# A hybrid decoder step: four buffers for raw weight blocks instead of three, and 64 tile slots instead of 66

## The chip, the cores and the metric

The kernel runs on one core of a Trainium2 chip. The metric is device time in microseconds of one execution; three executions of the kernel before took 2662.25, 2661.33 and 2662.22 us, so the median is 2662.22. The core has five engines with a queue each: TensorE (PE, with its weight loads shown as PEld), VectorE (DVE), ScalarE (ACT), GpSimd (POOL) and SyncE (SP). SP does nothing here but issue transfers; POOL issues a second stream of them.

## The reference

One layer of a decoder trunk in float32. The 512 tokens of a prompt and 8 tokens of a decode batch go through it together (520 columns in the kernel); d_model is 2048.

```python
def block(x, rg_h, rg_conv, C, n, m, ml_conv, mk, mv, w):
    y, new = mixer(rmsnorm(x, w['g_mix']), rg_h, rg_conv, C, n, m, ml_conv, w)
    x = x + y.astype(x.dtype)
    x = x + cross_attn(rmsnorm(x, w['g_xattn']), mk, mv, w).astype(x.dtype)
    hf = rmsnorm(x, w['g_ffn'])
    x = x + (jnp.square(jax.nn.relu(hf @ w['w_up'])) @ w['w_down']).astype(x.dtype)
    return x, new
```

The mixer multiplies by w_in (2048 x 5128) and feeds eight heads of a gated linear recurrence (RNN) and four heads of an mLSTM with a matrix state C (256 x 256 for each head; decode has a state of its own for each of 8 sequences), then multiplies by w_out. Cross-attention has four heads over 256 memory tokens: the prompt's keys and values are the memory times w_mk and w_mv, those of decode come from a cache (K, V). The feed-forward part has 8192 hidden columns: w_up, squared ReLU, w_down. Outputs are the two y and all the new states.

## The kernel before, in words

**Blocks and jobs.** All weights are cut into blocks of 128 partitions x 8 x 128 float32, 512 KB each. A list `jobs` has an entry for each product with a block. A float32 block is used as two halves: `whi`, cast to the type fp32r by ScalarE (line 129, or 138 where the order is written by hand), and `wlo`, block minus `whi`, by VectorE (line 130 or 146). The matmuls of a job are made three times, whi by xh, whi by xl, wlo by xh. So each job of w_in has 48 matmuls of 260 columns (line 205), a job of w_mk 24 (line 1100), and one of w_mv 12 of 512 columns (line 1131).

**How a block arrives.** `w_raw` (line 106) takes a raw buffer from `wpool` (line 60, three buffers for each tag) and has SP load the block (line 108). `run_jobs` (line 164) goes through the jobs: at job i it asks for the raw blocks of later jobs (`w_load`), for the blocks of a group of products five jobs ahead (`w_fetch`, FETCH = 5), makes the two halves for job i+2, steps through the running tasks (pieces of vector work between the matmuls), and then issues the matmuls of job i. SP's queue is in order: a load for which no raw buffer is free makes everything behind it wait.

**Groups of seven products.** w_out, w_co, w_up and w_down are taken four blocks at a time (A11, A12, A21, A22) with seven products instead of eight, from sums of blocks (`form`, line 1303) and sums of activations; their jobs (`quad_jobs`, matmuls in line 1333) use `fetch0` and `fetch1` to load A11 and A12 by `w_raw` and A21 and A22 into another pool of five buffers (line 1291). There a raw buffer comes free when VectorE has formed the last sum that reads it or the low half of it.

**Slots.** Nearly all other tiles of the size of an activation (up to 524 float32 for each partition) share one pool of slots (`slots`, SLOTS buffers). Activations of the hidden layer are written to memory (`hc`, lines 1362 and 1363) and read back in w_down (`ha`, `hact_load`, line 1506) together with the residual X (line 1534).

**Order of work.** Three stretches are in the order in which the program is written (`manual_schedule`): the prologue with the first 10 jobs, the w_cq, w_mk and w_mv jobs with cross-attention and the first w_co jobs (about 745 to 1220 us), and the end. All others are put in order by the framework's scheduler, with a priority that `tc.high_priority(offset=AHEAD)` raises for loads and halves. The stages in time: w_in with RNN and mLSTM to about 590 us; w_out to 745; w_cq to 940; w_mk and w_mv with attention to about 1170; w_co to about 1350 (with a gap at 1207 to 1216, where it waits for the attention of decode); w_up to about 1990; w_down to about 2640; the final norm.

**Lines that the text names.** RNN gates: matmuls in line 730, sigmoid `g` in 731, its tanh and exp in 735 and 736. mLSTM of the prompt: 656 and 659 (numerator and denominator), 663 (state update), 667 (state C on VectorE), 673 (`rd`, absolute value of the denominator). mLSTM decode: `ct`, scaled on ScalarE in 574 and stored as output. Attention: 224 (three-pass products), 1182 (p), 1195 (transpose of p), 1087 (`mvl`, low half of values), 1137 (`mv` from PSUM), 1138 (its store), 987 (decode's cached V, loaded by POOL), 799 (`to`, from which w_co is multiplied).

Of the kernel before, what the change touches and what calls it, by code (L numbers as in the profile page):

```python
# [9 lines left out]
F32 = mybir.dt.float32  # L10
# [7 lines left out]
P = 128  # L18
# [6 lines left out]
EPS = 1e-6  # L25
FF = 8192
NMEM = 256
SLOTS = 66
SLOT = 524

C_MIX, C_X, C_FFN, C_FIN, C_MEM = 0, 16, 32, 48, 64
# [14 lines left out]
def tile_trunk(ctx: ExitStack, tc: tile.TileContext, a, o):  # L46
# [3 lines left out]
    const = ctx.enter_context(tc.tile_pool(name="const", bufs=1))  # L50
    slots = ctx.enter_context(tc.tile_pool(name="slots", bufs=SLOTS))
    wpool = ctx.enter_context(tc.tile_pool(name="wpool", bufs=3))
# [11 lines left out]
    def nm(s):  # L64
        uid[0] += 1
        return f"{s}_{uid[0]}"
# [37 lines left out]
    tasks = []  # L104

    def w_raw(src):
        raw = wpool.tile([P, 8, P], F32, tag="wraw", name=nm("wraw"))
        load(raw, src)
        return raw

    def w_load(i):
        if "fetch" in jobs[i] or "raw" in jobs[i] or "w" in jobs[i]:
            return
        jobs[i]["raw"] = w_raw(jobs[i]["src"])

    def w_fetch(i):
        if i < len(jobs) and "fetch" in jobs[i]:
            jobs[i]["fetch"]()
# [22 lines left out]
    def w_low(i):  # L141
        if "w" in jobs[i]:
            return
        raw, hi = jobs[i].pop("cast")
        lo = wpool.tile([P, 8, P], F32R, tag="wlo", name=nm("wlo"))
        V.tensor_tensor(out=lo, in0=raw, in1=hi.bitcast(F32), op=ALU.subtract)  # L146
        jobs[i]["w"] = hi, lo
# [5 lines left out]
    def step_tasks(cost=1.0):  # L153
        for t in list(tasks):
            t[2] += 1.0 if t[1] is None else t[1] * cost
            while t[2] > 0.999:
                t[2] -= 1.0
                try:
                    next(t[0])
                except StopIteration:  # L160
                    tasks.remove(t)
                    break

    def run_jobs(first, last, fixed=False, low_first=False):


        n = len(jobs)
        for i in range(first, last):
            with tc.high_priority(offset=AHEAD):
                for k in (i + 3, i + 4)[1 if i else 0:]:  # L170
                    if k < n:
                        w_load(k)
                w_fetch(i + FETCH)
                if i + 2 < n:
                    (w_cast if fixed else w_split)(i + 2)
            j = jobs[i]
            if "pre" in j:
                j["pre"]()
            if low_first:
                w_low(i + 2)  # L180
            step_tasks(j.get("cost", 1.0))
            if fixed and i + 2 < n:
                w_low(i + 2)
            j["mm"](*j.pop("w"))
            if "post" in j:
                with tc.high_priority(offset=EVAC):
                    j["post"]()
        while last == n and tasks:
            step_tasks()
# [1092 lines left out]
    def quad_jobs(srcs, acts, nacc, evac, order=None, early=False):  # L1282
# [11 lines left out]
        def fetch0():  # L1294
            q["A11"] = w_raw(srcs[0])
            q["A21"] = raw2("A21", srcs[2])

        def fetch1():
            q["A12"] = w_raw(srcs[1])
            q["A22"] = raw2("A22", srcs[3])  # L1300
# [349 lines left out]
    with tc.manual_schedule():  # L1650
        prologue()
        run_jobs(0, EARLY)
    run_jobs(EARLY, n_cq)
    with tc.manual_schedule():
        run_jobs(n_cq, n_early + 2, True)
        while tasks:
            step_tasks()
# [117 lines left out]
```

## Time and profile before

| | |
|---|---|
| median of three executions | 2662.22 us |
| the profiled execution | 2666.71 us |
| its span | 2664.9 us |
| mean granted TensorE clock | 0.995 |
| TensorE matmuls busy | 2625.3 us (99%) |
| VectorE busy | 2222.9 us (83%) |
| ScalarE busy | 1297.3 us (49%) |
| read from memory, written | 434.26 MB, 103.59 MB |

The profile is of one execution. Busy time counts an engine's instructions; "waits" are idle stretches of an engine, put down to what ended them; the chain is the work that ended last, followed back. Matmuls overlap one another, so a matmul's own duration (some 280 to 400 ns) is longer than the distance between two of them.

### The profile page before, as it was taken

The numbers are of one execution on the slowest core, as the hardware profiler recorded it, in microseconds if no ns is written. First come the engines' busy times: TensorE is split into PE (matmuls) and PEld (weight loads), VectorE is DVE, ScalarE is ACT, GpSimd is POOL, SyncE is SP. The second block draws the span as 40 slices with busy tenths as digits, with TensorE's granted clock in tenths as the row PEclk, the third lists the DMA queues.
The fourth block names the chain that finished last, engine by engine and source line by source line (L and its number), as shares of the span: only waits on it lengthen the run. The fifth ranks groups of instructions, "written<-read, shape, count | busy, mean of one in ns | idle before, by whom it ended". The sixth has DMA issues, their size and how long they took to land.

```text
span 2664.9 us, 52682 instructions
## 1 busy us (share of the span) xinstructions
PE 2625.3 (99%) x21250; PEld 2588.0 (97%) x21250; DVE 2222.9 (83%) x3733; ACT 1297.3 (49%) x1783; POOL 125.5 (5%) x216
## 2 busy tenths in 40 slices
PE   9999999999999999998999999999999999999997
PEld 9999999999999988988999999999999999999997
DVE  6787685897865567879999999999999988998898
ACT  5646455553453145545565555555553333333344
POOL 0010010000001212320000000000000000000001
PEclk9999999999999999999999999999999999999999
DMA  5354343566455778886686565565579666555642
GB/s 199 111 183 155 112 167 102 177 221 236 141 186 200 272 269 274 293 282 221 219 273 242 199 211 183 199 211 185 197 244 329 217 222 217 185 171 186 214 129 89
DMA packets 241926, 541.17 MB, mean 203 GB/s; under 512 B 25630, under 2 KB 97982, under 8 KB 241682
## 3 DMA queue, kind: packets, MB, share of 16 engines
q1 hardware_dynamic: 221202, 466.42, 51.6%
q0 software_dynamic: 20480, 71.38, 7.8%
q8 instruction: 167, 2.74, 0.4%
q14 instruction: 77, 0.63, 0.1%
HBM read 434.26 MB, written 103.59 MB: 202 GB/s over the span
## 4 chain that ended last, share of the span: by engine, by line
PE 89%; DVE 5%; DMA 3%; issue 2%; ACT 1%; POOL 0%; SPq 0%; POOLq 0%; ACTq 0%; DVEq 0%
PE mm L1333 53%; PE mm L205 22%; PE mm L1100 3%; PE aux L1333 2%; PE aux L224 2%; PE mm L1131 2%; PE mm L1376 2%; DVE wlo L130 1%; DMA wraw<-in_w_mv 1%; ACT whi L129 0%; PE aux L730 0%; DVE wlo L146 0%; DMA hc<-r 0%; PE aux L663 0%; PE aux L659 0%
## 5 line engine op out<-in xcount | busy, mean ns | idle before, releaser
L129 ACT CAST whi<-wraw 128x1024 fp32r<-128x1024 f32 x396 | 416.1, 1051 | 637.0 <-PE mm L1333 422.9
L1333 PE MATMUL mm<-ha,whi 128*128 128x260 f32 x3584 | 643.7, 283 | 2.2 <-DVE X L1514 1.2
L130 DVE TENSOR_TENSOR wlo<-wraw,whi 128x1024 fp32r<-128x1024 f32 x396 | 483.6, 1221 | 121.4 <-ACT whi L129 116.1
L1333 PEld LDWEIGHTS mm<-ha,whi 128*128 128x128 f32 x3584 | 551.2, 188 | 3.1 <-DVE X L1514 1.6
L1333 PE MATMUL mm<-ha,wlo 128*128 128x260 f32 x1792 | 505.1, 282 | 0.5 <-DVE wlo L130 0.5
L1333 PE MATMUL mm<-ta,whi 128*128 128x260 f32 x2320 | 419.3, 283 | 0.0
L1333 PEld LDWEIGHTS mm<-ta,whi 128*128 128x128 f32 x2320 | 355.6, 188 | 0.1
L1333 PEld LDWEIGHTS mm<-ha,wlo 128*128 128x128 f32 x1792 | 336.9, 188 | 1.0 <-DVE wlo L130 0.9
L1333 PE MATMUL mm<-ta,wlo 128*128 128x260 f32 x1160 | 326.4, 281 | 0.0
L1333 PE MATMUL mm<-fa,whi 128*128 128x260 f32 x1488 | 269.8, 283 | 0.0
L205 PE MATMUL mm<-xh,whi 128*128 128x260 f32 x1280 | 265.2, 288 | 0.0
L205 PE MATMUL mm<-xl,whi 128*128 128x260 f32 x1280 | 259.3, 284 | 0.0
L205 PE MATMUL mm<-xh,wlo 128*128 128x260 f32 x1280 | 258.3, 283 | 0.0
L129 ACT CAST whi<-A 128x1024 fp32r<-128x1024 f32 x140 | 146.9, 1050 | 195.3 <-PE mm L1333 123.3
L1333 PEld LDWEIGHTS mm<-fa,whi 128*128 128x128 f32 x1488 | 229.2, 189 | 0.0
L138 ACT CAST whi<-wraw 128x1024 fp32r<-128x1024 f32 x100 | 105.1, 1051 | 239.0 <-PE mm L205 79.4
L1333 PEld LDWEIGHTS mm<-ta,wlo 128*128 128x128 f32 x1160 | 218.5, 188 | 0.0
L1333 PE MATMUL mm<-fa,wlo 128*128 128x260 f32 x744 | 209.7, 282 | 0.0
L1514 DVE TENSOR_TENSOR X<-mm,X 128x260 f32<-128x260 f32 x448 | 171.0, 422 | 41.4 <-PE mm L1333 38.7
L205 PEld LDWEIGHTS mm<-xh,whi 128*128 128x128 f32 x1280 | 198.7, 189 | 1.4
L205 PEld LDWEIGHTS mm<-xh,wlo 128*128 128x128 f32 x1280 | 198.4, 189 | 0.2
L205 PEld LDWEIGHTS mm<-xl,whi 128*128 128x128 f32 x1280 | 198.0, 189 | 0.4
(435 smaller groups left out, 5217.2 us busy)
## 6 DMA issues: line engine op xcount, KB each, us to landing
ha<-hc SPq DMA_DIRECT2D x224, 260.0 KB
wraw<-in_w_in SPq DMA_DIRECT2D x80, 512.0 KB
wraw<-in_w_up SPq DMA_DIRECT2D x66, 512.0 KB
wraw<-in_w_down SPq DMA_DIRECT2D x64, 512.0 KB
A<-in_w_down SPq DMA_DIRECT2D x64, 512.0 KB
A<-in_w_up SPq DMA_DIRECT2D x62, 512.0 KB
hc<-hhi SPq DMA_DIRECT2D x32, 910.0 KB
hc<-r SPq DMA_DIRECT2D x32, 910.0 KB
```

What stands on the lines that cost most here:

```text
L129: S.copy(hi, raw)
L130: V.tensor_tensor(out=lo, in0=raw, in1=hi.bitcast(F32), op=ALU.subtract)
L138: S.copy(hi, raw)
L205: PE.matmul(ps[:, hf, 0:HT], w[:, j, :], x[:, HALF[hf]], start=(k == 0 and wi == 0), stop=(k == n - 1 and wi == 2))
L224: PE.matmul(out, u, v, start=first and i == 0, stop=last and i == 2)
L1100: PE.matmul(box["ps"], w[:, i, :], x, start=(k == 0 and wi == 0), stop=(k == KB - 1 and wi == 2))
L1131: PE.matmul(box["ps"][:, i], x[:, ms], w[:, j], start=(k == 0 and wi == 0), stop=(k == KB - 1 and wi == 2))
L1333: PE.matmul(out, w[:, j, :], x[:, b], start=(new and k == 0 and wi == 0), stop=(p == LAST[acc] and k == per - 1 and wi == 2), skip_group_c ...
L1376: PE.matmul(ps[mp][:, hf, 0:HT], w[:, j, :], x[hf][:, b], start=(kp == 0 and j == 0 and wi == 0), stop=(kp == 1 and j == 7 and wi == 2))
L1514: V.tensor_tensor(out=x, in0=c, in1=x, op=ALU.add)
```

## The change

The raw blocks get four buffers in place of three (`bufs=4` in `w_raw`). `run_jobs` asks for the raw block of job i+5 where it asked for that of job i+4 (at job 0, where it asked for blocks 3 and 4, it asks for 3, 4 and 5). A buffer of a raw block is 4096 bytes in each partition; two slots of 524 float32 are 4192 bytes, and SLOTS goes from 66 to 64.

```diff
--- before.py
+++ after.py
@@ -25,7 +25,7 @@
 EPS = 1e-6
 FF = 8192
 NMEM = 256
-SLOTS = 66
+SLOTS = 64
 SLOT = 524
 
 C_MIX, C_X, C_FFN, C_FIN, C_MEM = 0, 16, 32, 48, 64
@@ -104,7 +104,7 @@
     tasks = []
 
     def w_raw(src):
-        raw = wpool.tile([P, 8, P], F32, tag="wraw", name=nm("wraw"))
+        raw = wpool.tile([P, 8, P], F32, tag="wraw", name=nm("wraw"), bufs=4)
         load(raw, src)
         return raw
 
@@ -167,7 +167,7 @@
         n = len(jobs)
         for i in range(first, last):
             with tc.high_priority(offset=AHEAD):
-                for k in (i + 3, i + 4)[1 if i else 0:]:
+                for k in (i + 3, i + 4, i + 5)[2 if i else 0:]:
                     if k < n:
                         w_load(k)
                 w_fetch(i + FETCH)
```

Which buffer a load waits for doesn't change: with three buffers block i+4 follows block i+1, with four block i+5 does.

Three places show how the order moves. First SP, where w_mk ends and w_mv begins (about 950 us). `wraw` are raw blocks, `dq` rearranges q for decode. Before:

```order
L108 DMA wraw_11489<-in_w_mk 128x1024
L108 DMA wraw_11529<-in_w_mk 128x1024
L965 DMA dq_11541<-qkd_11539 8x512
L108 DMA wraw_11570<-in_w_mk 128x1024
L108 DMA wraw_11604<-in_w_mv 128x1024
L108 DMA wraw_11639<-in_w_mv 128x1024
L108 DMA wraw_11676<-in_w_mv 128x1024
L108 DMA wraw_11713<-in_w_mv 128x1024
```

And with the change, at the same row of the queue:

```order
L108 DMA wraw_11455<-in_w_mk 128x1024
L108 DMA wraw_11491<-in_w_mk 128x1024
L108 DMA wraw_11531<-in_w_mk 128x1024
L965 DMA dq_11543<-qkd_11541 8x512
L108 DMA wraw_11572<-in_w_mv 128x1024
L108 DMA wraw_11606<-in_w_mv 128x1024
L108 DMA wraw_11641<-in_w_mv 128x1024
L108 DMA wraw_11678<-in_w_mv 128x1024
```

Each load stands one load earlier: `dq` now has the first w_mv block right behind it, in the place where the last of w_mk was.

Second SP, where w_up ends and w_down begins (about 1970 us). `hc` are stores of hidden activations, `ha` their loads, `A_` blocks A21 and A22. Before:

```order
L108 DMA wraw_23559<-in_w_up 128x1024
L1362 DMA hc_180<-hhi_23529 128x7x260
L1363 DMA hc_180<-r_23250 128x7x260
L108 DMA wraw_23771<-in_w_down 128x1024
L1291 DMA A_3084_23773<-in_w_down 128x1024
L1291 DMA A_3093_23819<-in_w_down 128x1024
L1506 DMA ha_23811<-hc_152 128x520
L1506 DMA ha_23813<-hc_153 128x520
L1506 DMA ha_23815<-hc_154 128x520
L1506 DMA ha_23852<-hc_151 128x520
L1506 DMA ha_23854<-hc_152 128x520
L108 DMA wraw_23817<-in_w_down 128x1024
```

With the change:

```order
L108 DMA wraw_23771<-in_w_down 128x1024
L1362 DMA hc_180<-hhi_23529 128x7x260
L1363 DMA hc_180<-r_23250 128x7x260
L1291 DMA A_3084_23773<-in_w_down 128x1024
L108 DMA wraw_23817<-in_w_down 128x1024
L1291 DMA A_3093_23819<-in_w_down 128x1024
L1506 DMA ha_23769<-hc_154 128x520
L1506 DMA ha_23809<-hc_151 128x520
L1506 DMA ha_23811<-hc_152 128x520
L1506 DMA ha_23813<-hc_153 128x520
L1506 DMA ha_23815<-hc_154 128x520
L1506 DMA ha_23852<-hc_151 128x520
```

The second `wraw` of w_down, which stood between `ha` loads, goes ahead of them. `ha_23769` and `ha_23809` weren't in this burst before: they were the last of six `ha` loads issued together at about 1455 us, of which four are left there.

Third the w_in stage, at about 480 to 500 us. TensorE around the matmuls of one chunk of an mLSTM head (lines 656 to 663), before:

```order
L205 MATMUL mm_6077<-xl_285,whi_5816 128x260 x2
L205 MATMUL mm_6077<-xh_284,wlo_5817 128x260 x2
L656 MATMUL aux_6132<-E_5467,tn_5640 128x128
L659 MATMUL aux_6132<-qs_5830,C_5834 128x128
L659 MATMUL aux_6132<-qs_5831,C_5835 128x128
L656 MATMUL aux_6132<-E_5467,tn_5640 128x128
L659 MATMUL aux_6132<-qs_5830,C_5834 128x128
L659 MATMUL aux_6132<-qs_5831,C_5835 128x128
L656 MATMUL aux_6132<-E_5467,ones 128x128
L659 MATMUL aux_6132<-qs_5830,C_5834 128x128
L659 MATMUL aux_6132<-qs_5831,C_5835 128x128
L663 MATMUL aux_6142<-tn_5640,tn_5729 128x257
```

With the change:

```order
L205 MATMUL mm_6079<-xh_311,wlo_5897 128x260 x2
L205 MATMUL mm_6079<-xh_315,whi_5896 128x260 x2
L205 MATMUL mm_6079<-xl_316,whi_5896 128x260 x2
L656 MATMUL aux_6134<-E_5469,tn_5642 128x128
L659 MATMUL aux_6134<-qs_5832,C_5836 128x128
L659 MATMUL aux_6134<-qs_5833,C_5837 128x128
L656 MATMUL aux_6134<-E_5469,tn_5642 128x128
L659 MATMUL aux_6134<-qs_5832,C_5836 128x128
L659 MATMUL aux_6134<-qs_5833,C_5837 128x128
L656 MATMUL aux_6134<-E_5469,ones 128x128
L659 MATMUL aux_6134<-qs_5832,C_5836 128x128
L659 MATMUL aux_6134<-qs_5833,C_5837 128x128
```

The nine matmuls from line 656 on stood behind the last matmul with block `whi_5816`; now they stand 17 rows, or 34 matmuls, later, in the middle of the next block (`whi_5896`, before `whi_5894`).

ScalarE at the same place, before:

```order
L715 ACT_TABLE_LOAD
L715 ACTIVATE gt_5999<-gt_5999 128x520
L574 ACTIVATE ct_6037<-ct_6037,bc 128x256 x2
L731 ACT_TABLE_LOAD
L731 ACTIVATE g_6059<-aux_6060,par 128x260
L731 ACTIVATE g_6059<-aux_6063,par 128x260
L129 CAST whi_6128<-wraw_5892 128x1024
L574 ACTIVATE ct_6039<-ct_6039,bc 128x256 x2
L731 ACTIVATE g_6066<-aux_6067,par 128x260
L731 ACTIVATE g_6066<-aux_6070,par 128x260
L673 ACTIVATE rd_6150<-aux_6132 128x128
L735 ACTIVATE tau_6073<-g_6059,spn 128x520
```

With the change:

```order
L129 CAST whi_6130<-wraw_5816 128x1024
L715 ACT_TABLE_LOAD
L715 ACTIVATE gt_6001<-gt_6001 128x520
L574 ACTIVATE ct_6039<-ct_6039,bc 128x256 x2
L731 ACT_TABLE_LOAD
L731 ACTIVATE g_6061<-aux_6062,par 128x260
L731 ACTIVATE g_6061<-aux_6065,par 128x260
L574 ACTIVATE ct_6041<-ct_6041,bc 128x256 x2
L673 ACTIVATE rd_6152<-aux_6134 128x128
L731 ACTIVATE g_6068<-aux_6069,par 128x260
L731 ACTIVATE g_6068<-aux_6072,par 128x260
L735 ACTIVATE tau_6075<-g_6061,spn 128x520
```

The cast of the next block moved from behind the first pair of gates to the row ahead of line 715 (its raw tile has another number, as it is asked for one job sooner), and `rd` from behind the second pair of gates to the place ahead of it.

## Rows read from the trace of the kernel before

**Rows 1.** The page's first part: busy time of each engine, its share of the span, number of instructions.

```profile
PE 2625.3 (99%) x21250; PEld 2588.0 (97%) x21250; DVE 2222.9 (83%) x3733; ACT 1297.3 (49%) x1783; POOL 125.5 (5%) x216
```

**Rows 2.** Table of stages: from:to and length in us; busy time (and number of instructions) of PE, PEld, DVE, ACT, POOL; mean granted TensorE clock; share of the DMA engines; GB/s. The stages that the text speaks of, without the four between them.

```profile
0.00:30.00 30.00, 26.46 (x166) 24.96 (x167) 19.00 (x41) 17.28 (x26) 0.20 (x4) 0.89 0.86 307
400.00:500.00 100.00, 97.54 (x784) 95.11 (x784) 67.47 (x146) 51.43 (x86) 5.69 (x12) 1.00 0.42 135
940.00:990.00 50.00, 48.96 (x324) 44.14 (x323) 33.62 (x61) 20.07 (x27) 8.93 (x14) 1.00 0.79 274
1200.00:1220.00 20.00, 9.34 (x63) 9.16 (x64) 16.36 (x31) 10.69 (x20) 0.00 (x0) 0.76 0.49 164
1220.00:1990.00 770.00, 769.50 (x6426) 768.98 (x6425) 712.23 (x930) 434.20 (x537) 0.00 (x0) 1.00 0.63 215
1990.00:2020.00 30.00, 28.26 (x234) 27.85 (x233) 27.31 (x37) 13.72 (x15) 0.00 (x0) 1.00 1.05 363
2020.00:2580.00 560.00, 560.00 (x4687) 559.85 (x4687) 503.02 (x699) 205.57 (x197) 0.00 (x0) 1.00 0.61 205
2640.00:2664.90 24.90, 11.42 (x83) 10.36 (x82) 16.30 (x39) 8.40 (x18) 8.42 (x12) 0.78 0.45 171
```

**Rows 3.** TensorE's waits by line and releaser (us in total, times, longest), first in the stretch 945 to 985 us (one row), then in 1110 to 1200 us (three rows).

```profile
PE mm L1131 <- DVE wlo L146: 1.0, 2, 0.5
...
PE mm L1131 <- DVE wlo L146: 2.4, 3, 1.7
...
PE aux L1195 <- DVE p L1182: 1.0, 1, 1.0
...
PE aux L224 <- DVE mvl L1087: 0.8, 1, 0.8
```

**Rows 4.** Timelines of TensorE (two rows) and ScalarE (two rows) at the w_mv blocks: start us, duration of the row, engine, line, operation, tiles, and in brackets the idle time before it and its releaser.

```profile
1153.83 0.50 PE L1131 MATMUL mm<-wlo,mh 128*128 128x512 f32 x1 [0.25 <-DVE wlo L146]
...
1158.61 0.50 PE L1131 MATMUL mm<-wlo,mh 128*128 128x512 f32 x1 [1.72 <-DVE wlo L146]
...
1150.33 1.05 ACT L138 CAST whi<-wraw 128x1024 fp32r<-128x1024 f32 x1 [3.20 <-DMA wraw<-in_w_mv]
...
1155.11 1.05 ACT L138 CAST whi<-wraw 128x1024 fp32r<-128x1024 f32 x1 [3.21 <-DMA wraw<-in_w_mv]
```

**Rows 5.** The chain that ended last, in order of time (start, us, engine, what): four steps between 959 and 1171 us; and two rows of POOL's timeline.

```profile
959.96 7.67 DMA wraw<-in_w_mv
...
1146.26 8.75 DMA wraw<-in_w_mv
...
1158.61 2.84 PE mm L1131 x11
...
1170.68 7.15 DMA kv<-in_V
...
1168.02 1.23 POOL L1138 DMA_DIRECT2D out_mv<-mv  x2 [6.68 <-ACT mv L1137]
1169.40 0.73 POOL L987 DMA_DIRECT2D kv<-in_V  x1 [0.15 <-issue]
```

**Rows 6.** The table of stages for five shorter stretches, with the same columns.

```profile
945.00:975.00 30.00, 28.96 (x193) 26.04 (x193) 21.27 (x41) 13.82 (x19) 8.93 (x14) 1.00 0.90 314
1130.00:1140.00 10.00, 9.00 (x49) 7.41 (x49) 7.72 (x21) 5.77 (x14) 3.75 (x7) 1.00 0.70 262
1140.00:1180.00 40.00, 38.04 (x207) 32.23 (x206) 28.75 (x87) 19.55 (x39) 13.99 (x24) 1.00 0.96 329
2000.00:2010.00 10.00, 9.90 (x83) 9.69 (x82) 8.42 (x14) 5.29 (x5) 0.00 (x0) 1.00 1.05 397
1210.00:1220.00 10.00, 3.34 (x15) 3.37 (x16) 8.16 (x16) 6.71 (x13) 0.00 (x0) 0.51 0.77 248
```

**Rows 7.** TensorE's waits in the stretch 400 to 500 us (four rows), and two rows of ScalarE's timeline there.

```profile
PE aux L663 <- ACT g L731: 0.8, 1, 0.8
PE aux L256 <- DVE hsq L268: 0.6, 1, 0.6
PE aux L730 <- DVE C L667: 0.6, 1, 0.6
PE aux L656 <- ACT g L731: 0.5, 1, 0.5
...
490.74 1.28 ACT L731 ACT_TABLE_LOAD   x1 [1.48 <-DMA out_s_C<-ct]
...
499.91 1.28 ACT L736 ACT_TABLE_LOAD   x1 [2.77 <-DMA out_s_C<-ct]
```

**Rows 8.** TensorE's waits in the stretch 1200 to 1220 us.

```profile
PE mm L1333 <- ACT to L799: 9.4, 1, 9.4
```

**Rows 9.** The waits of SyncE's own queue (SP) over the whole span.

```profile
SPq L108 <- DVE wraw L1303: 420.9, 66, 9.5
```

**Rows 10.** The start of the down projection: TensorE's waits in 1990 to 2020 us (two rows), one row of SP's timeline from further ahead (x6 is the number of transfers issued), and two rows of the page's sixth part (transfers by kind, number, KB each, median us to landing).

```profile
PE mm L1333 <- ACT whi L129: 1.0, 1, 1.0
PE mm L1333 <- DVE X L1514: 0.7, 1, 0.7
...
1455.55 2.96 SPq L1506 DMA_DIRECT2D ha<-hc  x6
...
ha<-hc SPq DMA_DIRECT2D x224, 260.0 KB
...
wraw<-in_w_down SPq DMA_DIRECT2D x64, 512.0 KB
```

## The prediction, made before the changed kernel ran

> **What bounds the kernel now.** I read the page's busy times first: TensorE's matmuls fill 99% of the span, VectorE 83% [rows 1]. So the change can only give back what TensorE idles, some 40 us, and it can only touch the part of them that a weight block's transfer causes. The table of stages shows where they lie [rows 2]: 2.5 us between 400 and 500 us, 1.0 between 940 and 990, 10.7 between 1200 and 1220, 1.7 between 1990 and 2020, 13.5 in the last 25; and between 1140 and 1180 us 2.0 of 40 [rows 6]. In the two long stretches from w_co on it loses 0.5 of 770 us and nothing of 560.
>
> Then TensorE's waits by releaser. Near 960 us (w_mk ends, w_mv begins) it waits 1.0 us for VectorE's low part of a block, and between 1110 and 1200 us 2.4 us in three waits for the same [rows 3]. Its timeline shows the two among those that a transfer can have caused, 0.25 and 1.72, before the w_mv matmuls at 1153.83 and 1158.61; ScalarE's casts just ahead of them had stood 3.20 and 3.21 us for the raw block's DMA [rows 4]. The chain of waits runs through the same transfers, 7.67 us at 959.96 and 8.75 us at 1146.26 [rows 5]. These 3.0 us (1.0 + 0.25 + 1.72) are the direct price of blocks that land late. The third wait (2.4 − 1.97 = 0.4) and the waits for p and mvl (1.0 and 0.8) are vector chains inside the attention, and stay.
>
> **The change part by part.**
> *The fourth buffer and the earlier transfer, w_mk and w_mv.* At job i the block of job i+5 is asked for instead of i+4, into the buffer that block i+1 frees; each transfer is queued one job sooner, as the order of SP at the end of w_mk shows. The condition it waits for at a given job is the one it had, the low part of block i+1, so nothing behind it on SP waits longer. A w_mv job is 12 matmuls, of which eleven took 2.84 us [rows 5], so a block begins at least some 3 us sooner. That is more than the longest TensorE wait (1.72) and about ScalarE's (3.2). What works against it is the load on the DMA engines: their share is 0.90 from 945 to 975 and 0.96 (329 GB/s) from 1140 to 1180, and 0.70 just before, from 1130 to 1140 [rows 6]. A transfer that starts earlier there runs beside others. The free share ahead, 0.30 × 10 = 3 us of all engines, or 3 × 329 GB/s = 1 MB, is two blocks; so the first late blocks can be pulled in and the later ones only partly. I take 2.0 of the 3.0, with 0 and 3.0 as ends.
>
> Is this gain kept? Between 1160 and 1200 us the next limit is the decode V stream. Its last loads stand in POOL's queue behind the store of mv, which waited 6.68 us for mv's eviction [rows 5], so they come forward with the w_mv jobs; the stall of 9.4 us that follows, for `to` from ScalarE (the attention's output as w_co multiplies it, decode columns last) [rows 8], is the end of that chain and moves forward whole. So I pass the gain on at full value.
>
> The Trainium skill ("DMA: Bandwidth & Descriptors", Specifications) gives about 358 GB/s as a NeuronCore's HBM limit, which would speak against the change; its section "Bandwidth" has 425 for a large transfer of one core alone. The trace shows 397 GB/s from 2000 to 2010 us [rows 6], so the lower figure isn't the ceiling here. By it the 40 us of the stage (329 × 40 = 13.2 MB) could shrink to no less than an estimated 36.8 us, which leaves room for all 3.0; the term stays.
>
> *First stage (30 to 745 us), reordered by the scheduler.* Raw blocks in a different place change priorities, and at 480 to 500 us instructions move on TensorE and ScalarE (the third place shown with the change). TensorE waits there 0.8 us (second product into the state, L663), 0.6 (the RNN gates' product, L730) and 0.5 (L656): 1.9 in all [rows 7]. The 0.6 for hsq at L256 stays. In the new order the L656 group stands 17 rows, 34 matmuls, later. At the steady rate, 560.00 us for 4687 matmuls or 0.12 us each [rows 2], that is 4.1 us more for its inputs, so its wait goes, and L730 is likewise behind more matmuls. The wait of L663 goes only in part: it needs a PSUM buffer that the second pair of gates frees, and that pair now stands on ScalarE behind rd, which itself needs the L659 products just ahead. I take 1.2 of 1.9. Ends: all 1.9 gained; 1.5 lost, since on ScalarE two scalings of ct now precede the gates elsewhere too, and for a store of such a tile ScalarE waited 1.48 ahead of 490.74 [rows 7].
>
> *The groups of seven products.* SP waited 420.9 us in 66 stretches for a raw buffer to come free [rows 9]; this queue time will shrink greatly. It's covered: TensorE hardly idles there [rows 2], because the blocks land long before their casts. What queues behind a load on SP (hidden stores, ha loads, A blocks) can move a few us at no price. I take 0, with the 0.5 us now lost as the gain's end. Without this cover a load that came as late as the longest SP wait, 9.5 us, would show in TensorE's waits already.
>
> *Down start (1990 to 2020 us).* TensorE waits 1.0 for a cast and 0.7 for X, in a stretch where the DMA engines are full, 397 GB/s at a share of 1.05 [rows 6, 10]. The raw block that stood between ha loads now goes ahead of them: 512 KB leave the burst. But with 64 slots two ha loads that the trace has in the group of six at 1455.55 us now wait until the burst: 2 × 260 = 520 KB come in [rows 10]. The bytes ahead of X are equal. I take 0. Ends: 1.7 gained, if the cast's block and X both come in time; 1.3 lost, if the 520 KB delay X at 397 GB/s and the block's move doesn't help.
>
> *The two slots fewer.* Everywhere else slots cost only if a tile waits for one; in 1220 to 1990 us TensorE lost 0.5, so 0, within the ends above. *Start and end.* The first loads come in another order at 18 us, in a stretch where TensorE is busy 26.46 of 30 us and the granted clock is 0.89 [rows 2]; the blocks of the first four jobs are asked for in either order ahead of their casts; the last 25 us have no weight blocks. 0.
>
> **Sum.** −2.0 − 1.2 + 0 + 0 + 0 = −3.2 us. Against the profiled execution's own time, 2666.71 (span 2664.9 and 1.8 around it), that is 2663.5. The runs shown have a median of 2662.22, 4.49 below the profiled one; taken from there it is 2659.0. The ends added up: 0 + 1.5 + 1.3 = +2.8 at worst, −3.0 − 1.9 − 0.5 − 1.7 = −7.1 at best, without knock-on effects.
>
> **Rivals.**
> *A: the DMA engines are the limit of the w_mv stage, and the earlier start only stretches each transfer.* For it: 0.96 of 1.0 in 1140 to 1180; the 512 KB of a block took 8.75 us there. Against: 0.70 just before. Then the 2.0 becomes 0: 2662.2 − 1.2 = 2661.0.
> *B: all waits on a transfer go, and the transition follows.* 3.0 + 1.9 + 1.7 = 6.6; the V transfer on the chain, 7.15 us [rows 5], finds fewer raw blocks beside it and takes some 5 (it then moves 512 KB at the rate of the stage with one block less), 2 more; and a shorter stall brings TensorE sooner off the lower of its two clock levels (1.2 GHz; 0.51 granted in 1210 to 1220) [rows 6], some 1.9 of the 4 us at that level from 1216. −10.5: 2651.7. Against: each part must go the whole way.
> *C, slower: the first stage loses.* On ScalarE an operation on the decode state ct, whose buffer waits on a store, stands ahead of the gates that TensorE waits for; ScalarE stood 1.48 and 2.77 us behind such a store ahead of its table loads at 490.74 and 499.91 [rows 7]. Two to three such places among the eight heads' gates, not covered by matmuls, cost 4 to 8 us. It decides once it exceeds the 2.0 + 1.2 of the forecast: with 6 and A's absent gain, 2662.2 + 6 = 2668; with the 2.0 kept, 2666. For it: VectorE's and ScalarE's orders change in over a hundred lines there. Against: TensorE's order barely does, and its idle in 400 to 500 is only 2.5 us with the same mix.
> *D: nothing happens,* as the buffer is still freed by the same low part, and a transfer that starts 3 us sooner only lands 3 us sooner before a cast that had its block: 2662. For it: 99% busy.
>
> **How the numbers follow.** Forecast (−1.5 to −5) 0.40, A 0.17, B 0.13, C 0.12, D 0.18. The likeliest gives 2659.0. For a range that leaves out 2 in 10 I go from B's middle to C's beginning: 2652 to 2666. About 0.2% (5.3 us) is what a measurement of this kernel can tell from no change: faster beyond it are B and the lower fifth of the forecast and a share for couplings not priced, 0.25; slower is most of C, 0.10; the rest, 0.65, within.
>
> **What would show it right or wrong.** In the changed profile TensorE's waits for the low part (L146) at 945 to 985 and 1110 to 1200 fall from 3.4 to about 1.4, and ScalarE's waits on the w_mv transfers with them; in 480 to 500 the waits at L656 and L730 are gone; 1990 to 2020 loses 1.7 still; SP's waits for a raw buffer fall by over half with no effect on the feed-forward stretches. Wrong would be: new TensorE waits of over 1 us in 30 to 745; the stall at 1207 longer by what the w_mv stage gained; or the end of up_quad losing time to late ha loads.

## The result, and the profile after

The changed kernel takes 2673.57 us (median of 4, 2672.91 to 2674.51), the kernel before on the same chip 2661.77 us: a ratio of 1.0041, 95% interval 1.0026 to 1.0056 (the two medians alone give 1.0044). It is 11.8 us slower, where 3.2 us faster was forecast, and lies above the range. The profiled execution took 2674.51 us, its span is 2672.7. The medians in this document leave out three executions far above the others (3728.81 us of the slots alone, 3652.32 of four buffers with 66 slots, 9075.54 of the kernel before), and each ratio is to executions of the kernel before that were timed beside the run.

Busy times hardly tell [rows 1]: TensorE does the same 21250 matmuls, in 2630.9 us where it was 2625.3.

The table of stages of the changed kernel finds the place (same columns as [rows 2]; the long stretches are moved by the 8 to 10 us by which it is later there).

```profile
500.00:600.00 100.00, 94.22 (x744) 93.32 (x743) 84.44 (x163) 58.91 (x91) 1.07 (x2) 0.95 0.54 177
545.00:565.00 20.00, 19.49 (x163) 19.31 (x162) 20.00 (x41) 14.47 (x26) 0.00 (x0) 1.00 0.51 159
565.00:585.00 20.00, 14.73 (x108) 14.55 (x107) 18.34 (x34) 9.96 (x15) 0.00 (x0) 0.83 0.90 293
...
500.00:503.00 3.00, 3.00 (x16) 3.00 (x15) 1.66 (x6) 0.91 (x2) 0.00 (x0) 0.50 0.43 168
...
1150.00:1190.00 40.00, 40.00 (x224) 34.73 (x223) 31.21 (x95) 21.35 (x42) 14.17 (x24) 1.00 0.96 339
1230.00:2000.00 770.00, 769.70 (x6429) 769.19 (x6428) 711.34 (x929) 434.51 (x537) 0.00 (x0) 1.00 0.63 214
2000.00:2030.00 30.00, 28.96 (x241) 28.63 (x240) 27.67 (x39) 13.64 (x14) 0.00 (x0) 1.00 1.05 366
```

And two rows of the same table for the kernel before:

```profile
500.00:600.00 100.00, 100.00 (x827) 99.65 (x827) 89.14 (x174) 60.36 (x96) 1.08 (x2) 1.00 0.60 199
...
545.00:565.00 20.00, 20.00 (x169) 20.00 (x168) 19.96 (x40) 12.51 (x23) 0.00 (x0) 1.00 0.49 161
```

Before, TensorE was busy throughout from 500 to 600 us; now 5.8 us are missing, nearly all between 565 and 585, and the granted clock of those 20 us is 0.83. VectorE is full in the 20 us ahead (20.00 us), as it was before (19.96). The stretch from 1230 to 2000 loses 0.3 (0.5 before, in [rows 2]), the down start 1.0 of 30 (1.7 before). The stage of w_mv is better: no idle time at all from 1150 to 1190, where 1140 to 1180 had lost 2.0 [rows 6], at the same share of the DMA engines, 0.96.

How much each stage gives and takes is read from a timeline of TensorE grouped by operands, whose rows give the first and the last start of a group (after the three durations). `fy,whi` begins w_out, `mh,whi` of line 1100 begins w_mk, `fo,whi` begins w_co. Before:

```profile
L1376 PE MATMUL mm<-fy,whi x128: 277/282/287, 587.6 to 610.1; 128*128 128x260 f32 x128
L1376 PE MATMUL mm<-fo,whi x128: 277/282/328, 1169.6 to 1198.9; 128*128 128x260 f32 x128
...
L1100 PE MATMUL mm<-mh,whi x256: 277/281/365, 938.4 to 1107.3; 128*128 128x256 f32 x128
```

After:

```profile
L1376 PE MATMUL mm<-fy,whi x128: 277/282/288, 599.0 to 621.6; 128*128 128x260 f32 x128
L1376 PE MATMUL mm<-fo,whi x128: 277/283/387, 1177.2 to 1206.5; 128*128 128x260 f32 x128
...
L1100 PE MATMUL mm<-mh,whi x256: 274/281/366, 950.3 to 1117.5; 128*128 128x256 f32 x128
```

w_out begins 11.4 us later (587.6 to 599.0; a second profile of the kernel before, shown below, has 584.7, so this figure is good to some 3 us). From the start of w_mk to that of w_co it took 231.2 us (1169.6 − 938.4) and takes 226.9 (1177.2 − 950.3): 4.3 us come back. At the first matmul of w_co the kernel is 7.6 us late, and 7.8 at the end of the span. That pair of executions understates the loss, because the profiled execution of before was 4.9 us above its median and that of after only 0.9.

What is new before 600 us are TensorE's waits (in us: in total, times, longest). The first row is of 500 to 600 us, the next two of 280 to 500, the last of 940 to 1200:

```profile
PE mm L205 <- DVE og L777: 5.8, 2, 5.3
...
PE aux L256 <- DVE hsq L268: 1.9, 2, 1.5
PE aux L656 <- ACT g L731: 1.9, 1, 1.9
...
PE mm L1131 <- DVE wlo L146: 0.5, 1, 0.5
```

The first one matters. On TensorE's timeline (start, duration of the row, number of matmuls, idle time before and its releaser):

```profile
568.33 0.40 PE L205 MATMUL mm<-xh,wlo 128*128 128x260 f32 x2
574.00 0.77 PE L205 MATMUL mm<-xh,whi 128*128 128x260 f32 x2 [5.27 <-DVE og L777]
574.58 0.64 PE L205 MATMUL mm<-xl,whi 128*128 128x260 f32 x2
575.01 0.64 PE L205 MATMUL mm<-xh,wlo 128*128 128x260 f32 x2
...
578.04 0.43 PE L205 MATMUL mm<-xh,whi 128*128 128x260 f32 x2
```

TensorE stops at 568.73 (568.33 + 0.40) and waits 5.27 us for line 777, VectorE's evacuation of an output-gate block into the tile `og`: an evacuation moves a finished sum out of PSUM, the memory that the matmuls write their sums to (`mm`), and TensorE needs one of the two PSUM buffers (`pmm`) of w_in to go on. When it does, two matmuls take 0.43 us (574.58 to 575.01) at the lower of the two clock levels (1.2 GHz): nine pairs take 4.04 us, from 574.00 to 578.04, where at the steady 0.12 us a matmul they take 2.2, so 1.9 us more. VectorE's rows for `og`, with the instruction ahead of the late one:

```profile
507.62 0.70 DVE L777 TENSOR_TENSOR og<-mm,rssq 128x520 f32<-128x520 f32 x1 [0.42 <-PE aux L659]
...
556.15 0.69 DVE L777 TENSOR_TENSOR og<-mm,rssq 128x520 f32<-128x520 f32 x1
...
572.71 0.41 DVE L819 TENSOR_TENSOR kv<-gt,kv 128x260 f32<-128x260 f32 x1
573.16 0.70 DVE L777 TENSOR_TENSOR og<-mm,rssq 128x520 f32<-128x520 f32 x1
```

And in the kernel before:

```profile
504.51 0.69 DVE L777 TENSOR_TENSOR og<-mm,rssq 128x520 f32<-128x520 f32 x1
...
547.35 0.70 DVE L777 TENSOR_TENSOR og<-mm,rssq 128x520 f32<-128x520 f32 x1
...
561.76 0.70 DVE L777 TENSOR_TENSOR og<-mm,rssq 128x520 f32<-128x520 f32 x1
...
570.06 0.69 DVE L777 TENSOR_TENSOR og<-mm,rssq 128x520 f32<-128x520 f32 x1
```

Between the last two evacuations lie 17.0 us (556.15 to 573.16) where the kernel before had 14.4, and then 8.3; TensorE fills a PSUM buffer in 96 matmuls, 11.5 us at 0.12 each. One distance above 11.5 costs nothing here, as there is a second buffer; it is the sum that tells. From the first row to the late one are four distances, 65.5 us with the change and 5.8 of waiting, and 57.3 before (504.51 to 561.76) without any. VectorE wasn't idle: in its row at 573.16 it has no wait in brackets, it was simply placed there, right behind a row of line 819 that reads a `gt` tile. The chain of waits runs mostly through VectorE from 536 us to the stall and then back to TensorE, all of it in places where the chain of before was TensorE alone:

```profile
563.12 2.04 DVE kv L819 x6
...
574.00 25.11 PE mm L205 x192
```

The two smaller waits, for hsq (line 268) and for the gates (line 731), are 1.9 us each; with 0.4 for C they make 4.2, where the waits of the stage made 2.5 before [rows 7]. Idle time thus rises by 5.8 + 1.7, and the lower clock behind the long stop adds 1.9. Behind the wait for the gates the clock falls too: it is 0.50 from 500 to 503 us (the row of the table of stages above), and the 18 matmuls from 499.16 to 503.02 take 3.9 us where the next group of the same kind, from 505.79, takes 2.0: 1.9 us more. Together that is 11.3 of the 11.4 us.

Of the rest: ScalarE's wait for the w_mv transfers fell from 11.4 us in 1094 to 1192 to 5.0 in 1094 to 1202, and SP's waits for a raw buffer in the groups of seven [rows 9] from 420.9 only to 391.5:

```profile
ACT whi L138 <- DMA wraw<-in_w_mv: 5.0, 3, 1.9
```

```profile
SPq L108 <- DVE wraw L1303: 391.5, 50, 9.6
```

At the down start the wait for X (0.7 in [rows 10]) is gone and the one for the cast is what it was, 1.0 us. The second profile of the kernel before has no wait for X there either.

### The profile page after: what moved, and what is told of

Its sections match the earlier page's. It is cut to its first block, busy times and chain, and to the rows that moved or that the text cites. A ratio compares the mean times of both kernels' runs of the same rounds, so it can differ in the third digit from the quotient of the medians.

```text
span 2672.7 us, 52718 instructions
## 1 busy us (share of the span) xinstructions
PE 2630.9 (98%) x21250; PEld 2595.0 (97%) x21250; DVE 2224.7 (83%) x3733; ACT 1298.0 (49%) x1783; POOL 125.4 (5%) x216
## 4 chain that ended last, share of the span: by engine, by line
PE 85%; DVE 6%; issue 5%; ACT 2%; DMA 2%; POOL 1%; SPq 0%; POOLq 0%; DVEq 0%; ACTq 0%
PE mm L1333 52%; PE mm L205 20%; PE mm L1100 3%; PE aux L1333 2%; PE aux L224 2%; PE mm L1131 2%; PE mm L1376 2%; DVE wlo L130 1%; PE aux L730 0%; DMA ct<-in_C 0%; PE aux L659 0%; DVE kv L1019 0%; ACT whi L129 0%; PE aux L663 0%; DVE wlo L146 0%
```

## The experiments

Theory S: the two slots fewer, not the raw buffers, slow the w_in stage, and they do so by the evacuation `og`, which needs a slot. Rival R: the raw blocks' new place in the scheduler's order does it. Whether the gain in the w_mv stage is real is a question of its own.

**Slots alone.**

```diff
-SLOTS = 66
+SLOTS = 64
```

> SLOTS = 64 alone, with three raw buffers and the old lookahead. Theory S (the loss is the two slots: in the w_in stage the og tile, which takes a slot, is evacuated late, and TensorE waits for its PSUM buffer): the 5.3 us wait of TensorE for og at about 568 us is there, w_out starts some 11 us later than before (599 in place of 587.6), and the time is at or above the changed kernel's, 2673 to 2678. Rival R (the raw blocks' new place in the scheduler's order causes it): no such wait, w_out starts at 588, time 2662 within 2.

Measured: 2677.03 us (three executions) against 2664.23 before on that chip, ratio 1.0046 (1.0029 to 1.0063), 12.8 us slower with three raw buffers and the old lookahead. TensorE's waits in 500 to 600 us (first row) and in 1990 to 2030 (second):

```profile
PE mm L205 <- DVE og L777: 5.8, 2, 5.3
...
PE mm L1333 <- DVE X L1514: 2.3, 1, 2.3
```

```profile
L1376 PE MATMUL mm<-fy,whi x128: 277/282/288, 597.3 to 619.9; 128*128 128x260 f32 x128
L1376 PE MATMUL mm<-fo,whi x128: 277/282/369, 1177.8 to 1207.1; 128*128 128x260 f32 x128
...
L1100 PE MATMUL mm<-mh,whi x256: 274/281/367, 948.7 to 1116.9; 128*128 128x256 f32 x128
```

The wait for `og` is there, 5.8 in all as after, w_out begins at 597.3, 9.7 later than before. R falls. The order says the same: in the traces TensorE's instructions through the whole of w_in are the changed kernel's, one for one, and the two differ only in the place of one group of w_down. So the order of w_in was made by the slots. The run is slower than the changed kernel, as it lacks the fourth buffer's gain (1177.8 − 948.7 = 229.1 us from w_mk to w_co, where the changed kernel takes 226.9), and at the down start it waits 2.3 us for X. That may be the price of the two ha loads that come late. It is one profile; with 64 slots and the fourth buffer, with or without the earlier request, no wait for X is seen there.

**Buffers, without the earlier request.**

```diff
-SLOTS = 66
+SLOTS = 64
...
-        raw = wpool.tile([P, 8, P], F32, tag="wraw", name=nm("wraw"))
+        raw = wpool.tile([P, 8, P], F32, tag="wraw", name=nm("wraw"), bufs=4)
```

> 64 slots and four raw buffers, but each load asked for where it was before (job i+4). Theory S with SP held by buffers alone: the place of the request doesn't matter where SP waits for a buffer, so this is the changed kernel again, 2672 to 2675, with the gain in the w_mv stage. If the earlier request is what brings that gain (rival), the waits for the low part near 1155 stay and the time is some 2 to 4 us above the changed kernel, 2676 or more.

Measured: 2672.75 us, ratio 1.0032 (1.002 to 1.0045); from w_mk to w_co 1176.7 − 949.9 = 226.8 us.

```profile
L1376 PE MATMUL mm<-fo,whi x128: 277/282/393, 1176.7 to 1206.1; 128*128 128x260 f32 x128
...
L1100 PE MATMUL mm<-mh,whi x256: 274/281/367, 949.9 to 1116.9; 128*128 128x256 f32 x128
```

The stage is the changed kernel's within 0.1 us: the fourth buffer brings the gain, and asking a job earlier brings nothing there. That SP stands waiting for a buffer, so that the buffer's release and not the place of the request sets when a transfer begins, fits this; it wasn't followed transfer by transfer. The whole time agrees less closely, 8.5 us over the kernel before beside it where the changed kernel has 11.8, but the two intervals overlap. Set against the run with the slots alone, the buffers are worth 2677.03 − 2672.75 = 4.3 us.

**og without a slot.** The changed kernel with one line edited; `xr_tile()` gives one of the two buffers that hold the residual in w_out and are idle until then.

```diff
     def ev_og(i):
         def ev(ps):
-            t = slot("og")
+            t = xr_tile()
```

> The changed kernel, with the tile og taken from the two xr buffers (idle in that stage) in place of a slot. Theory S, with og's slot as the mechanism: the wait of 5.3 us for og is gone and with it the stretch at the lower clock behind it; w_out starts 8 to 11 us earlier than in the changed kernel, time 2662 to 2666. If VectorE's backlog and not the slot makes og late: w_out starts at 597 or later and the time stays at 2671 or above.

Measured: 2663.23 us, ratio to before 0.9998 (0.9989 to 1.0008), about 10 us faster than the changed kernel's 2673.57 (which was timed beside runs of the kernel before that were 2.5 us faster), and 9.5 us faster than the run of the buffers alone, 2672.75, timed beside it. TensorE's instructions are the changed kernel's row for row. VectorE evacuates at distances of 12.4 and 10.5 us where the changed kernel had 17.0:

```profile
555.68 0.69 DVE L777 TENSOR_TENSOR xr<-mm,rssq 128x520 f32<-128x520 f32 x1
...
568.06 0.69 DVE L777 TENSOR_TENSOR xr<-mm,rssq 128x520 f32<-128x520 f32 x1
...
578.55 0.69 DVE L777 TENSOR_TENSOR xr<-mm,rssq 128x520 f32<-128x520 f32 x1
```

TensorE is busy through the 100 us (columns of the table of stages), and w_out begins at 589.8:

```profile
500.00:600.00 100.00, 100.00 (x814) 99.41 (x813) 90.58 (x176) 63.24 (x102) 1.08 (x2) 0.99 0.61 197
```

```profile
L1376 PE MATMUL mm<-fy,whi x128: 277/282/290, 589.8 to 612.4; 128*128 128x260 f32 x128
```

So the long stop doesn't come from the order of TensorE; it comes from the late `og`, and that was late for want of a slot. It isn't shown which tile held that slot, and as the edit leaves the other tiles a slot more, the want is shown and not whose it was. VectorE's backlog, the rival here, falls: with the same work to do it evacuates in time. Some 3 us of the loss in w_in stay, for the gates (1.9 us of waiting, and 0.50 of the clock in 500 to 502) and for hsq (1.5), and eat most of what the buffers gain.

**The kernel before once more.**

> The kernel before, unchanged, profiled once more: it tells whether the waits at 960 and 1155 us and the execution's 2666.7, 4.5 above its median, belong to the kernel or to that execution. If to the execution: 2661 to 2663 in this profile, with the w_mv waits for the low part under 1.5 us in all; if to the kernel: 2665 to 2667 with 3.4 again.

Measured: median 2663.89 us beside 2664.23 for the kernel before in the same runs, ratio 0.9998 (0.9987 to 1.0008); profiled at 2664.64. TensorE's waits for the low part in 940 to 1200 us:

```profile
PE mm L1131 <- DVE wlo L146: 3.2, 3, 1.4
```

3.2 us again, so these waits belong to the kernel and not to one execution. The time fell between the two forecasts, which settles nothing by itself. It also shows how far one profile can be trusted: the same kernel, but w_out begins 2.9 us earlier than in the first profile.

```profile
L1376 PE MATMUL mm<-fy,whi x128: 277/282/287, 584.7 to 607.3; 128*128 128x260 f32 x128
```

**Four buffers with all 66 slots.** The memory is taken elsewhere.

```diff
-        raw = wpool.tile([P, 8, P], F32, tag="wraw", name=nm("wraw"))
+        raw = wpool.tile([P, 8, P], F32, tag="wraw", name=nm("wraw"), bufs=4)
...
-                for k in (i + 3, i + 4)[1 if i else 0:]:
+                for k in (i + 3, i + 4, i + 5)[2 if i else 0:]:
...
-        qkd = sm("qkd", (NB, 512))
+        qkd = sm("qkd", (NB, 512), 1)
...
-        wg = sm("wg", (P, 2, P))
+        wg = sm("wg", (P, 2, P), 1)
...
-        qd = sm("qkd", (NB, 512))
+        qd = sm("qkd", (NB, 512), 1)
...
-        pd = sm("pd", (NB, NMEM))
+        pd = sm("pd", (NB, NMEM), 1)
...
-tag="wq", name=nm(name), bufs=5)
+tag="wq", name=nm(name), bufs=4)
```

> Four raw buffers and the earlier load with all 66 slots: the memory comes from one buffer less for A21 and A22 (four in place of five) and from second buffers of qkd, pd and wg. Theory S: the w_in stage is as in the kernel before (no wait of 5 us for og, w_out reached at the same distance from the start within 1 us), the w_mk and w_mv stage is 4 us shorter as in the changed kernel, and nothing else moves: 3 to 5 us faster than before, ratio 0.998 to 0.999. Rival T (the fourth buffer gains nothing that lasts; the 4 us were an accident of the profiled executions): ratio 1.000. Rival U (the buffer missing for A21 and A22 costs in the groups of seven): new TensorE waits after 1220 us, ratio over 1.001.

Measured: 2661.36 us against 2664.25 before, ratio 0.9989 (0.9981 to 0.9998): 2.9 us faster, the only kernel here whose interval lies below 1, if barely. Its table of stages:

```profile
500.00:600.00 100.00, 100.00 (x828) 99.66 (x827) 91.63 (x171) 58.60 (x95) 1.07 (x2) 1.00 0.64 210
945.00:975.00 30.00, 30.00 (x199) 27.37 (x198) 23.77 (x43) 14.81 (x19) 7.06 (x11) 1.00 0.99 354
1220.00:1990.00 770.00, 769.35 (x6427) 768.60 (x6426) 720.53 (x927) 432.92 (x536) 0.00 (x0) 1.00 0.66 215
```

w_in has no stall, 945 to 975 none either (1.0 before), and the long stretch of groups of seven loses 0.65 of 770 where it lost 0.5, so four buffers for A21 and A22 are enough. From w_mk to w_co it takes 1163.1 − 935.9 = 227.2 us:

```profile
L1376 PE MATMUL mm<-fo,whi x128: 277/282/345, 1163.1 to 1192.4; 128*128 128x260 f32 x128
...
L1100 PE MATMUL mm<-mh,whi x256: 277/281/365, 935.9 to 1103.2; 128*128 128x256 f32 x128
```

U falls, and with the same gain in all five profiles that have four buffers T does too.

**The same, with og out of the slots.** The edit of the third run on top of the fifth.

> As e5_four_and_66, and og in the two xr buffers as well, so that one slot more is free in the w_in stage than ever before. If slots are short only below 66, this equals e5 within 1.5 us; if the kernel before was already losing to slots there, it is 1 to 3 us faster than e5.

Measured: 2661.9 us, ratio 0.9992 (0.9983 to 1.0001); w_mk to w_co 226.9 us (1163.0 − 936.1, same view). The same as without it, within 0.5 us: at 66 slots `og` costs nothing, so the shortage begins below.

**One slot fewer.**

```diff
-SLOTS = 66
+SLOTS = 65
```

> The kernel before with 65 slots and nothing else. Theory S as a threshold: og's evacuation is already placed late once (in the order its distance to the one before is 37 rows in place of 29), so a wait of 2 to 6 us for og appears near 565 us and the time is 3 to 9 us above before. If the loss takes both slots: within 1.5 us of before.

Measured: 2671.47 us against 2664.25, ratio 1.0026 (1.0016 to 1.0036), 7.2 us slower. The wait for `og` is there, once and shorter, and not alone: TensorE also has a new wait at 489 us, for `hh` ahead of the gates' product (waits in 480 to 600 us).

```profile
PE mm L205 <- DVE og L777: 2.3, 1, 2.3
PE aux L730 <- DVE hh L677: 2.2, 1, 2.2
```

Behind both the granted clock falls (0.66 in 489 to 494, 0.89 in 565 to 580). So `og` is only a part of what the first slot costs. For that part the four distances of `og` add up to 61.8 us here (506.33 to 568.16, same view as above) and TensorE waits 2.3; with 64 slots it was 65.5 and 5.8. In both the sum exceeds the wait by 59.5 to 59.7 us, an estimate of what TensorE can stand; the kernel before, with 57.3, was then some 2 us from its first wait. With 66, 65 and 64 slots and three raw buffers the time over before is 0, 7.2 and 12.8 us.

## Why the prediction was wrong

**The step that failed** is "The two slots fewer. Everywhere else slots cost only if a tile waits for one; in 1220 to 1990 us TensorE lost 0.5, so 0". It looked at the feed-forward stretch and not at w_in, where the sentence's own condition was met. Its size is 12.8 us with three raw buffers, 7.2 for the first slot alone. The sign of being wrong that the prediction had named, new TensorE waits of over 1 us in 30 to 745, came: 5.3, 1.9 and 1.5.

**The first stage, −1.2,** had the wrong sign and the wrong cause. It put the moved instructions down to the raw blocks' priorities; the run with the slots alone has the same order of TensorE there. Of its three waits L730 shrank (0.6 to 0.4), L663 went, but L656 grew from 0.5 to 1.9: being later by 34 matmuls (4.1 us) on TensorE didn't help, since the gates that release it moved further: ScalarE's table load ahead of them starts at 497.33 where it stood at 490.74 [rows 7], 6.6 us later.

```profile
496.41 0.91 ACT L574 ACTIVATE ct<-ct,bc 128x256 f32<-128x256 f32 x2 [0.41 <-DMA ct<-in_C]
497.33 1.28 ACT L731 ACT_TABLE_LOAD   x1
```

And the place examined, 480 to 500 us, wasn't where most of the loss is: 568 us had no wait before and so no row. VectorE's order was never gone through for evacuations, though it has `og` 34 instructions after the one ahead of it where before it stood 29 after.

**Rival C** had the place (the first stage) and a fit size (+4 to 8, against +11.4 at the start of w_out), but its mechanism is the smaller part. It is seen at the gates: the scaling of ct at 496.41 waits for a load of ct, stands ahead of the table load for the gates, and TensorE's 1.9 us for them and the 1.9 at the lower clock follow. The larger part, 5.8 and 1.9, is evacuations on VectorE behind tasks, which no rival had. With C at 0.12, the range ended where it began.

**The w_mk and w_mv stage, −2.0,** was right in mechanism (a buffer more lets the blocks come sooner) and too small. Over all profiled executions the stage took 231.2, 233.4, 229.1 and 230.3 us with three buffers (before, before again, 64 slots, 65 slots), 231.0 on average, and 226.8 to 227.2 in the five with four: 4.0 us, above the upper end of 3.0. Waits for the low part fell from 3.4 to 0.5 us as forecast and further; the sum counted idle time alone, while by the distances of starts on TensorE's timeline a wait can cost some 0.16 us more (the matmuls around 1158.61 lie 1.88 us further apart than their neighbours where [rows 4] has 1.72). Rival A falls: with the share at 0.96 as before, the blocks came in time. The figure of 358 GB/s from the Trainium skill ("DMA: Bandwidth & Descriptors", Specifications) bound nothing: the rows show 339 GB/s in 1150 to 1190 and 366 at the down start.

**That the gain is passed on** held: the changed kernel is 7.6 us late at the first matmul of w_co and 7.8 at the end of the span (8.4 in between, at the start of line 1376's work with `fa`, 1353.6 before and 1362.0 after). **The groups of seven at 0** held, though SP's waits fell by 7% and not by over half; why is not shown, perhaps because one more buffer is soon full as well. **The down start at 0** held: 1.0 us of 30 is lost where it was 1.7. It may hide two parts, as the run with 64 slots alone waits 2.3 us for X and those with 64 slots and the fourth buffer don't.

**The earlier request** was counted as the cause of the earlier transfer. It is the buffer; in the stage the request changed nothing that can be measured (226.8 us without, 226.9 with).

## What to carry to other kernels

Where a change pays for buffers with tiles of a shared pool, the pool's tightest moment has to be found first: list what is alive there, and look in the new order at the evacuations of PSUM, add up the distances over a row of them and ask how long TensorE can go on filling buffers meanwhile (here an estimated 59.6 us for four distances, where the new order took 65.5). A stage without any wait in the old profile can hold the new bound, because an engine that is full throughout (VectorE, 20.00 of 20 us ahead of the stall, 19.96 before) needs only another order of the same work to become late. If a buffer is what a queue waits for, add the buffer and leave the request where it is.

## What the runs showed that wasn't expected

Three raw buffers give a w_mk to w_co stage of 229.1 to 233.4 us in four profiles of three kernels (231.2 and 233.4 for the same one), four buffers 226.8 to 227.2 in five profiles of five kernels: the fourth buffer seems to take out the scatter as well as the wait. And a short stop of TensorE can be dearer than it looks: the 5.27 us at 568 us were followed by 4 us at the lower clock, 1.9 us more, and the 1.89 us at 497 by another 1.9, as much as the wait itself. It isn't certain to follow: in the run without the earlier request the same wait of 1.89 us left the clock at 1.00 (498 to 503 us).
